# Norm weights per k tile on two engines, a running sum moved behind a K eviction, and V tiles drawn ahead of the memory attention, in the second layer of a two-layer trunk

## The chip, the cores and the metric

One core of a Trainium2 chip runs the whole program. The metric is the time of one execution on the device in microseconds (us), the median of three. Five instruction streams work side by side: TensorE (PE, with its weight loads as PEld), VectorE (DVE), ScalarE (ACT), GpSimd (POOL) and SyncE (SP), which issues the DMAs. Each takes its own instructions in order.

## The reference

Two layers over 1024 positions of width 1024. The change lies in layer B, whose front part computes this:

```python
h = rmsnorm(x, g_mix[l])
mem_k, mem_v = jnp.split(mem_n @ w_mem_kv[l], 2, axis=-1)
hk = rmsnorm(x, g_kv)
kvf = hk @ w_kvf                      # K (12 heads x 64), V (12 x 64), forget logits (12)
cum_logf = jnp.cumsum(jax.nn.log_sigmoid(f_logit), axis=1)
p = h @ w_in_b[l - N_A]               # FoX queries (12 heads) and memory queries (4 heads)
mix = forgetting_attention(q, k_sh, v_sh, cum_logf)
mem_o = memory_attention(q_mem, mem_k, mem_v)
x = x + jnp.concatenate([mix, mem_o], axis=-1) @ w_out[l]
x = x + conv_ffn(rmsnorm(x, g_ffn[l]), ...)
```

`rmsnorm(x, g)` scales by `g` along the width, which is the contracted dimension of each projection. So the norm weights can be multiplied into the weight matrix, and the row factor of the norm is applied to the result.

## The kernel before

Every operand of a float32 product is split into two parts, hi and lo, and a product is three matmuls: hi by hi, lo by hi, hi by lo (`mm3`, lines 108 to 110, and line 1111 for V). The width of 1024 is eight k tiles of 128 rows.

**Weights.** `load_w` (line 87) loads 128 x 1024 weights (for V 128 x 1040, half of a group of four heads) into one of two `raw` buffers. Where norm weights are given, one POOL multiply over the whole tile (line 99) applies them in place, ACT casts the product to hi (line 81) and DVE subtracts to get lo (line 82). Twenty loads in layer B do so: two memory-query tiles (`wqm`), six V halves (`wv`), six K tiles (`wk`), six Q tiles (`wq`).

**Order of the front part of layer B.** `normed` (line 178) splits x and, for each half of 512 positions, adds up squares, transposes the sum into columns by matmul (`st`, line 133), takes root and reciprocal (`sd` on ACT, `rs` on DVE, lines 140 and 142) and broadcasts the result back by matmul (`bc`, line 123), which ACT copies to `rb` (line 190). `st` and `bc` of both halves take the PSUM banks c2 and c3 in turn. `memattn(0)` projects the memory queries (`pq`, banks c0 and c1) and runs `mem_attention` (line 233): scale by `rb` (line 240), split (`bmq`, lines 246 and 247), scores (`ms`), softmax, transposes (`mt`) and values (`mo`).

**Fill.** Between those steps TensorE gets other work from a list: `mark` (line 290) pops steps from it at a given rate, `drain_fill(n)` pops n at once. During the memory attention the list holds 96 V steps (three groups of heads, eight token tiles each, four steps of six matmuls per tile, `vps`); each tile ends with an eviction by ACT and DVE (lines 1117 to 1120). Afterwards the list holds 192 K and Q steps (per pair of heads t: 8 K steps for the first half of the positions, 8 for the second, then 16 for Q), each of three matmuls; 32 of them are drained at once. For t = 0 the two halves use banks c0 and c1; from t = 1 on all use c0, so each half waits until the one before it is evicted by DVE (`bkc`, line 1170, and `bqc`, line 1172).

**Running sum.** The forget logits go through a chain of small DVE and ACT operations, are transposed (`lft`, line 1199), and summed along positions by one DVE scan (`bcum`, line 1204). ACT and DVE split the sum (`bch`, `bcl`, lines 1207 and 1208), four DMAs write it and its negative to memory, and `prep` loads them as extra rows of the score operands. After that, 20 more fill steps (`AHEAD`) are drained and the attention loop starts (`scores`, `values`: `fs`, `ft`, `fo`).

**Who sets the order.** The instructions are traced in the order of the program, and a scheduler that simulates the engines sorts each engine's stream; `issue_after(ins)` lets an instruction follow `ins` on its engine. So a change of the code also moves instructions that it doesn't name.

Of the kernel before, what the change touches and what calls it, by code (L numbers as in the profile page):

```python
# [8 lines left out]
F32 = mybir.dt.float32  # L9
# [3 lines left out]
ALU = mybir.AluOpType  # L13
AX = mybir.AxisListType

P = 128
# [14 lines left out]
VP = 260  # L31
# [20 lines left out]
class Trunk:  # L52
# [34 lines left out]
    def load_w(self, src, shape, gains=None, name="w", pools=None, lo_eng=None):  # L87

        nc = self.nc
        ph, pl = pools or ((self.main, "wh", None), (self.main, "wl", None))  # L90
        raw = self.main.tile([P] + shape, F32, tag="raw", name=f"{name}_raw", bufs=self.NRAW)
        nc.sync.dma_start(raw, src)
        hi = ph[0].tile([P] + shape, F32R, tag=ph[1], name=f"{name}_hi", bufs=ph[2])
        lo = pl[0].tile([P] + shape, F32R, tag=pl[1], name=f"{name}_lo", bufs=pl[2])
        if gains is None:
            self.split(hi, lo, raw, lo_eng=lo_eng)
        else:
            g = gains.rearrange("p (k o) -> p k o", o=1).to_broadcast([P] + shape)
            self.GENG(nc).tensor_tensor(raw, raw, g, op=ALU.mult)
            self.split(hi, lo, raw, lo_eng=self.LOENG(nc))  # L100
        return hi, lo

    def mm3(self, out, terms, start=True, stop=True):
# [930 lines left out]
    def layer_b(self):  # L1034
        nc, tc = self.nc, self.tc
# [3 lines left out]
        def pth(dt, nm):  # L1039
            return pc.tile([P, HS], dt, tag="pt", name=nm, bufs=6)  # L1040

        wqm = self.load_w(self.wib[CT], [KD, P], gains=self.vec("g_mix1", 0, KD), name="wqm0")
        xh, xl, rb, cols = self.normed("b", None, tmp1=lambda nm, w: pth(F32, nm))
# [4 lines left out]
        def unit(shape, dt, nm):  # L1048
            return self.main.tile(shape, dt, tag="x", name=f"b{nm}")

        def ptile(w=HS):
            return pc.tile([P, HS], F32, tag="ps", name="ps", bufs=4)[:, :w]

        def proj_half(w, u, hf, ks):
            wh, wl = w
            n = len(ks)
            self.mm3(u, [(wh[:, k], wl[:, k], xh[hf][k], xl[hf][k]) for k in ks],
                     start=ks[0] == 0, stop=ks[-1] == KD - 1)
# [7 lines left out]
        def memattn(ct):  # L1066
            w = wqm if ct == 0 else self.load_w(self.wib[CT + ct], [KD, P], gains=self.vec("g_mix1", 0, KD),
                                                name=f"wqm{ct}")
            hs = []
            for hf in range(2):  # L1070
                u = self.ps.tile([P, HS], F32, tag=f"c{hf}", name="pq")
                proj_half(w, u, hf, list(range(KD)))
                hs.append(u)
            o = [ptile(), ptile()]

            def put(e, hf, po):
                self.fold_rows(o[hf], po, e, self.nt("fr"))
                if e == 1:
                    nc.sync.dma_start(self.d_mix[CT + ct, :, hf * HS:(hf + 1) * HS], o[hf])

            self.mem_attention(hs, rb, ct, ks1, vs1, unit, pth, put, ("b2", "c2", "c3"), self.VMARKS)
# [8 lines left out]
        def load_v(pc_):  # L1090
            if pc_ < 3 and pc_ not in wv:
                wv[pc_] = [self.load_w(self.wv[pc_, u], [4, VP], gains=self.vec("g_kv", 4 * u, 4), name=f"wv{pc_}{u}",
                                       pools=((vp, "vh", 4), (vp, "vl", 4))) for u in range(2)]

        def v_steps(pc_):

            d = {}

            def step(i):
                t, kk = i // 4, i % 4  # L1100
                hf, ti = t // 4, t % 4
                if i == 0:
                    load_v(pc_ + 1)
                if kk == 0:
                    d["ps"] = self.ps.tile([P, VP], F32, tag=f"c{t % 2}", name="vps")
                ps = d["ps"]
                tsl = slice(ti * P, (ti + 1) * P)
                for k in (2 * kk, 2 * kk + 1):
                    wh, wl = wv[pc_][k // 4]
                    for j, (a, w) in enumerate(((xh, wh), (xl, wh), (xh, wl))):  # L1110
                        nc.tensor.matmul(ps, lhsT=a[hf][k][:, tsl], rhs=w[:, k % 4], start=k == 0 and j == 0,  # L1111
                                         stop=k == KD - 1 and j == 2)
                if kk == 3:
                    r = cols[hf][:, ti:ti + 1]
                    vo = vp.tile([P, 4, P], F32R, tag="vo", name="vo", bufs=3)
                    pv_ = ps[:, :MEM].rearrange("p (h d) -> p h d", h=4)
                    nc.scalar.activation(vo[:, :, :DH], pv_, AF.Copy, scale=r)
                    nc.vector.scalar_tensor_tensor(vo[:, :, DH:], pv_, r, vo[:, :, :DH].bitcast(F32),
                                                   op0=ALU.mult, op1=ALU.subtract)
                    nc.vector.scalar_tensor_tensor(fl[:, t, 4 * pc_:4 * pc_ + 4], ps[:, MEM:], r,  # L1120
                                                   self.bf[:, 4 * pc_:4 * pc_ + 4], op0=ALU.mult, op1=ALU.add)
                    nc.sync.dma_start(self.d_v[pc_, :, :, t], vo.bitcast(F32))
            return [lambda i=i: step(i) for i in range(32)]
# [12 lines left out]
        for e in range(2):  # L1136
            d = {n: pb.tile([P, S], F32R, tag=f"{n}{e}", name=f"{n}{e}") for n in ("q1", "q2", "k1", "k2")}
# [8 lines left out]
        def load(u):  # L1146
            t, n = u // 2, "kq"[u % 2]
            if t < CT and (t, n) not in ws:
                src, g = (self.wk, "g_kv") if n == "k" else (self.wib, "g_mix1")
                ws[t, n] = self.load_w(src[t], [KD, P], gains=self.vec(g, 0, KD), name=f"w{n}{t}")  # L1150
# [3 lines left out]
        def kq_steps(t):  # L1154

            d = kqv[t] = {}

            def step(i):
                n, hf, k = ("k", "q")[i // 16], i // 8 % 2, i % 8
                sl = slice(hf * HS, (hf + 1) * HS)  # L1160
                if i % 16 == 0:
                    load(2 * t + (n == "q") + 1)
                    d["w" + n] = ws.pop((t, n))
                    d[n] = unit([P, S], F32, n + "c")
                if k == 0:
                    d["u"] = self.ps.tile([P, HS], F32, tag="c1" if t == 0 and hf else "c0", name="pq")
                proj_half(d["w" + n], d["u"], hf, [k])
                if k == KD - 1:
                    if n == "k":
                        nc.vector.tensor_tensor(d[n][:, sl], d["u"], rb[:, sl], op=ALU.mult)  # L1170
                    else:
                        nc.vector.scalar_tensor_tensor(d[n][:, sl], d["u"], SCALE, rb[:, sl],
                                                       op0=ALU.mult, op1=ALU.mult)
            return [lambda i=i: step(i) for i in range(32)]
# [20 lines left out]
        lf = unit([NFOX, S], F32, "lf")  # L1195
# [5 lines left out]
        on = unit([NFOX, S], F32, "on")  # L1201
        nc.gpsimd.memset(on, 1.0)
        cum = unit([NFOX, S], F32, "cum")
        nc.vector.tensor_tensor_scan(cum, on, lf, 0.0, op0=ALU.mult, op1=ALU.add)
        ch = unit([NFOX, S], F32R, "ch")
        cl = unit([NFOX, S], F32R, "cl")
        nc.scalar.copy(ch, cum)
# [10 lines left out]
        def prep(t, e):  # L1218
            k, q = kqv[t]["k"], kqv[t]["q"]
            h = 2 * t + e  # L1220
            d = st[e]
            a, b = (slice(0, DH), slice(DH, P)) if e == 0 else (slice(DH, P), slice(0, DH))
            nc.vector.tensor_copy(d["q1"][a], q[a])
            nc.vector.tensor_copy(d["k1"][a], k[a])
            nc.gpsimd.tensor_tensor(d["q1"][b], q[a], d["q1"][a].bitcast(F32), op=ALU.subtract)
            self.dup2(d["k1"][b], d["k1"][a])
            nc.gpsimd.tensor_tensor(d["k2"][a], k[a], d["k1"][a].bitcast(F32), op=ALU.subtract)
            self.dup(d["q2"][a], d["q1"][a])
            e0 = DH if e == 0 else 0
            nc.sync.dma_start(d["q2"][e0:e0 + 2].bitcast(F32), self.d_c[h, 0:2])  # L1230
            nc.sync.dma_start(d["k2"][e0 + 2:e0 + 4].bitcast(F32), self.d_c[h, 2:4])
            vs = pb.tile([P, KD, P], F32R, tag="vsf", name="vsf", bufs=2)
            nc.sync.dma_start(vs.bitcast(F32), self.d_v[h // 4, :, h % 4])
            return vs
# [59 lines left out]
                    nc.tensor.matmul(po, lhsT=vs[:, j], rhs=pl[:, u], start=False, stop=j == 2 * I + 1)  # L1294
            self.fold_rows(o, po, e, self.nt("fr", 2 * P))

        self.drain_fill(self.AHEAD)
        vss = {(0, 0): prep(0, 0), (0, 1): prep(0, 1)}
        its = [(t, e, I) for t in range(CT) for e in range(2) for I in range(4)]
        pend = []  # L1300
# [125 lines left out]
    LAG = 2  # L1426
    VLAG = 3
    VRATE = 3.0
    GENG = staticmethod(lambda nc: nc.gpsimd)
    LOENG = staticmethod(lambda nc: nc.vector)  # L1430
    RATE = 0.8888888888888888
    LOOK = 1
    PREP = (5, 7)
# [135 lines left out]
```

## Time and profile before

| | us |
|---|---|
| median of three runs | 2347.88 |
| the runs | 2345.26, 2347.88, 2347.89 |
| the profiled execution | 2350.14 |
| its span, first to last instruction | 2348.3 |
| PE busy | 2261.3 (96%) |
| DVE, ACT, POOL busy | 1457.6, 1075.4, 1335.9 |
| mean granted TensorE clock | 0.987 of full |

The profiled execution took 1.84 us outside its span and lies 2.26 us above the median. All times in rows are us from the start of the span; durations in rows of single instructions are us, in rows of counts they are ns. A granted clock of 1.00 is 2.4 GHz, 0.50 is 1.2 GHz. A bracket at the end of a row is the time for which the engine sat idle before the instruction, and what it waited for.

### The profile page before, as it was taken

What the parts mean: (1) busy time and instruction counts of PE and PEld (TensorE: products, weight loads), DVE (VectorE), ACT (ScalarE), POOL (GpSimd) and SP (SyncE); (2) the same over time, 40 slices, a digit from 0 to 9 for tenths busy, and PEclk for the clock granted to TensorE, in tenths of its full rate; (3) what the DMA queues carried; (4) which work ended last, traced back from release to release, by engine and by line L of the source; (5) the groups of instructions that cost most, each with busy time, mean ns of one, the idle gap of its engine ahead of it and who ended that gap; (6) DMA issues with size and microseconds to landing.
All of it is one profiled execution on the core that took longest, in us unless ns stands there. A gap on an engine that the chain in (4) does not pass through costs nothing.

```text
span 2348.3 us, 29697 instructions
## 1 busy us (share of the span) xinstructions
PE 2261.3 (96%) x10970; PEld 1869.1 (80%) x10970; DVE 1457.6 (62%) x1995; ACT 1075.4 (46%) x1864; POOL 1335.9 (57%) x1003
## 2 busy tenths in 40 slices
PE   6999889999999999999998999999899999999998
PEld 6777668877878787888897888788788888778887
DVE  7479787766666653325645777866766666655225
ACT  6876746443434343223542666754443333343212
POOL 3676844566777776453423444614486767666533
PEclk9999989999999999999999999999999999999999
DMA  6100113222222235332432232433122222245322
GB/s 241 37 27 28 33 69 119 68 80 74 81 81 83 82 110 189 102 107 89 129 104 81 70 78 72 122 103 126 54 90 80 83 72 90 72 132 181 108 72 72
DMA packets 85281, 216.74 MB, mean 92 GB/s; under 512 B 9008, under 2 KB 29232, under 8 KB 85136
## 3 DMA queue, kind: packets, MB, share of 16 engines
q1 hardware_dynamic: 84992, 214.52, 28.7%
q8 instruction: 86, 1.41, 0.3%
q14 instruction: 59, 0.48, 0.1%
q10 hardware_dynamic: 144, 0.32, 0.0%
HBM read 156.94 MB, written 51.58 MB: 89 GB/s over the span
## 4 chain that ended last, share of the span: by engine, by line
PE 52%; DVE 4%; POOL 2%; issue 2%; DMA 2%; ACT 1%; DVEq 0%; ACTq 0%; POOLq 0%; SPq 0%
PE uY L345 7%; PE dn L109 7%; PE dn L108 6%; PE dn L110 6%; PE uX L345 5%; PE uV L345 5%; PE vps L1111 3%; PE pq L108 2%; PE pq L110 2%; PE pq L109 2%; DMA wd_raw<-in_wdn 1%; PE ft L1285 1%; PE fo L1294 1%; PE fo L1293 1%; PE fs L1249 1%
## 5 line engine op out<-in xcount | busy, mean ns | idle before, releaser
L345 PE MATMUL uY<-fT,fwh 128*128 128x512 f32 x1056 | 331.2, 394 | 5.9 <-DVE fuv L564 3.0
L109 PE MATMUL dn<-gl,wd_hi 128*128 128x512 f32 (+1 forms) x752 | 284.6, 379 | 0.5 <-POOL gl L82 0.5
L651 DVE TENSOR_TENSOR fx<-fx,dn 128x512 f32<-128x512 f32 (+1 forms) x176 | 111.2, 638 | 277.7 <-PE dn L110 276.3
L108 PE MATMUL dn<-gh,wd_hi 128*128 128x512 f32 (+1 forms) x752 | 280.7, 378 | 1.3 <-ACT fx L650 1.3
L110 PE MATMUL dn<-gh,wd_lo 128*128 128x512 f32 (+1 forms) x752 | 279.1, 375 | 0.0
L345 PEld LDWEIGHTS uY<-fT,fwh 128*128 128x128 f32 x1056 | 196.5, 188 | 55.8 <-DVE fuv L546 8.5
L345 PE MATMUL uX<-fB,fwh 128*128 128x512 f32 x704 | 223.0, 398 | 9.0 <-ACT fuv L521 9.0
L345 PE MATMUL uY<-fT,fwl 128*128 128x512 f32 x528 | 206.7, 391 | 0.0
L82 POOL TENSOR_TENSOR fwl<-wa,fwh 128x512 fp32r<-128x512 f32 x88 | 118.7, 1350 | 119.0 <-ACT fwh L81 119.0
L82 POOL TENSOR_TENSOR wd_lo<-wd_raw,wd_hi 128x1024 fp32r<-128x1024 f32 x44 | 108.0, 2461 | 127.5 <-ACT wd_hi L81 120.5
L345 PEld LDWEIGHTS uX<-fB,fwh 128*128 128x128 f32 x704 | 132.8, 190 | 42.0 <-ACT fuv L521 12.0
L108 PEld LDWEIGHTS dn<-gh,wd_hi 128*128 128x128 f32 x752 | 141.2, 188 | 30.0 <-ACT fx L650 1.7
L110 PEld LDWEIGHTS dn<-gh,wd_lo 128*128 128x128 f32 x752 | 141.0, 188 | 27.2
L109 PEld LDWEIGHTS dn<-gl,wd_hi 128*128 128x128 f32 x752 | 141.3, 188 | 25.8 <-POOL gl L82 0.9
L82 POOL TENSOR_TENSOR fwl<-wb,fwh 128x512 fp32r<-128x512 f32 x88 | 119.4, 1359 | 63.8 <-ACT fwh L81 63.0
L864 POOL TENSOR_TENSOR yp<-yp,ct 128x512 f32<-128x512 f32 x100 | 135.7, 1360 | 28.7 <-ACT ct L863 23.8
L82 POOL TENSOR_TENSOR gl<-g,gh 128x512 fp32r<-128x512 f32 x88 | 117.0, 1350 | 56.9 <-ACT gh L81 56.7
L82 POOL TENSOR_TENSOR fwl<-fs,fwh 128x512 fp32r<-128x512 f32 x88 | 118.3, 1346 | 52.9 <-ACT fwh L81 52.9
L345 PE MATMUL uX<-fB,fwl 128*128 128x512 f32 x352 | 138.5, 395 | 0.0
L345 PEld LDWEIGHTS uY<-fT,fwl 128*128 128x128 f32 x528 | 99.2, 188 | 22.4
L81 ACT CAST wd_hi<-wd_raw 128x1024 fp32r<-128x1024 f32 x44 | 45.6, 1050 | 152.4 <-issue 83.7
L345 PE MATMUL uV<-fB,fwh 128*128 128x512 f32 x352 | 111.5, 394 | 1.5 <-DVE fuv L529 1.5
(398 smaller groups left out, 6235.2 us busy)
## 6 DMA issues: line engine op xcount, KB each, us to landing
wb<-in_wup SPq DMA_DIRECT2D x44, 512.0 KB
wa<-in_wup SPq DMA_DIRECT2D x44, 512.0 KB
d_g<-fsg SPq DMA_DIRECT2D x44, 512.0 KB
wd_raw<-in_wdn SPq DMA_DIRECT2D x44, 512.0 KB
g<-d_g SPq DMA_DIRECT2D x44, 512.0 KB
d_x<-x SPq DMA_DIRECT2D x32, 256.0 KB
nxs<-d_x SPq DMA_DIRECT2D x32, 256.0 KB
wia_raw<-in_wia SPq DMA_DIRECT2D x14, 512.0 KB
```

Source lines behind the costliest of these rows:

```text
L81: nc.scalar.copy(hi, src)
L82: (lo_eng or nc.gpsimd).tensor_tensor(lo, src, hi.bitcast(F32), op=ALU.subtract)
L108: nc.tensor.matmul(out, lhsT=ah, rhs=bh, start=start and i == 0, stop=False)
L109: nc.tensor.matmul(out, lhsT=ah, rhs=bl, start=False, stop=False)
L110: nc.tensor.matmul(out, lhsT=al, rhs=bh, start=False, stop=stop and i == n - 1)
L345: mm = nc.tensor.matmul(out, lhsT=w[:, k], rhs=h[k], start=start and k == 0 and j == 0, stop=k == n - 1 and j == 2, skip_group_check=True)
L651: return nc.vector.tensor_tensor(self.x[m][:, sl], self.x[m][:, sl], ps, op=ALU.add)
L864: nc.gpsimd.tensor_tensor(y[:, hf], y[:, hf], c, op=ALU.add)
L1111: nc.tensor.matmul(ps, lhsT=a[hf][k][:, tsl], rhs=w[:, k % 4], start=k == 0 and j == 0, stop=k == KD - 1 and j == 2)
L1249: mm = nc.tensor.matmul(o, lhsT=d["q1"][:, qs], rhs=d["k1"][:, ksl], start=True, stop=False)
L1285: mm = nc.tensor.transpose(pt[:, u, P:], p1[:, j * P:(j + 1) * P], self.ident)
L1293: nc.tensor.matmul(po, lhsT=vs[:, j], rhs=ph[:, u], start=j == 0, stop=False)
```

## The change

`load_w` no longer multiplies the whole tile on POOL. For each k tile ACT computes hi with the norm weight as its scale (`split_gain`, line 168 before, 167 after) and DVE computes lo as x times weight minus hi (line 169 before, 168 after). Eight steps of the V fill, which are two tiles, are drained between the query projection and the memory attention, and the first two V tiles use banks c2 and c3. Eight K steps (the first half of t = 1) are drained before the running sum, and the scan is issued behind the eviction that ends them; 12 more steps follow the scan instead of 20.

```diff
         if gains is None:
             self.split(hi, lo, raw, lo_eng=lo_eng)
         else:
-            g = gains.rearrange("p (k o) -> p k o", o=1).to_broadcast([P] + shape)
-            self.GENG(nc).tensor_tensor(raw, raw, g, op=ALU.mult)
-            self.split(hi, lo, raw, lo_eng=self.LOENG(nc))
+            for k in range(shape[0]):
+                self.split_gain(hi[:, k], lo[:, k], raw[:, k], gains[:, k:k + 1])
         return hi, lo
...
                 hs.append(u)
+            if ct == 0:
+                self.drain_fill(8)
             o = [ptile(), ptile()]
...
                 if kk == 0:
-                    d["ps"] = self.ps.tile([P, VP], F32, tag=f"c{t % 2}", name="vps")
+                    d["ps"] = self.ps.tile([P, VP], F32, tag=f"c{t % 2 + 2 * (t < 2 and pc_ == 0)}", name="vps")
...
                     if n == "k":
-                        nc.vector.tensor_tensor(d[n][:, sl], d["u"], rb[:, sl], op=ALU.mult)
+                        self.last_k = nc.vector.tensor_tensor(d[n][:, sl], d["u"], rb[:, sl], op=ALU.mult)
...
         cum = unit([NFOX, S], F32, "cum")
-        nc.vector.tensor_tensor_scan(cum, on, lf, 0.0, op0=ALU.mult, op1=ALU.add)
+
+        self.drain_fill(8)
+        with self.issue_after(self.last_k.ins):
+            nc.vector.tensor_tensor_scan(cum, on, lf, 0.0, op0=ALU.mult, op1=ALU.add)
...
-        self.drain_fill(self.AHEAD)
+        self.drain_fill(self.AHEAD - 8)
...
-    GENG = staticmethod(lambda nc: nc.gpsimd)
-    LOENG = staticmethod(lambda nc: nc.vector)
```

What this does to the order of the engines is shown at three places. The first is PE at the end of the norm of layer B (`st` of the second half of the positions, its `bc`, the first scores `ms`). Before:

```order
L133 MATMUL st<-ones_69,sq 128x1 x4
L123 MATMUL bc<-ident,rs 128x128 x4
L259 MATMUL ms<-bks_8602,bmq 128x256
L260 MATMUL ms<-bks_8603,bmq 128x256
L259 MATMUL ms<-bks_8602,bmq 128x256
```

Now:

```order
L132 MATMUL st<-ones_69,sq 128x1 x4
L1112 MATMUL vps<-wv_hi,bh_8466 128x260
L1112 MATMUL vps<-wv_hi,bl_8482 128x260
L1112 MATMUL vps<-wv_lo,bh_8466 128x260
...
L1112 MATMUL vps<-wv_lo,bh_8473 128x260
L122 MATMUL bc<-ident,rs 128x128 x4
L258 MATMUL ms<-bks_8615,bmq 128x256
```

The 24 matmuls of the first V tile now stand between `st` and `bc`; eight `ms` follow `bc`, and then the second V tile. Before, the first V tile stood behind those eight `ms`.

The second place is ACT at the same time, where `sd` is the root that the second half's norm needs. Before:

```order
L152 ACTIVATE sq<-fx_6841 128x512
L81 CAST wv_hi<-wv_raw 128x1040
L190 COPY rb<-bc 128x512
L140 ACTIVATE sd<-st,eps_rms 128x4
L81 CAST wv_hi<-wv_raw 128x1040
```

Now:

```order
L151 ACTIVATE sq<-fx_6841 128x512
L167 ACTIVATE wv_hi<-wv_raw,vecs 128x260 x8
L189 COPY rb<-bc 128x512
L139 ACTIVATE sd<-st,eps_rms 128x4
L245 CAST bmq<-pq 64x512 x2
```

Both halves of the next V group (eight pieces) now stand ahead of `sd`; before it was one half.

The third place is DVE around the running sum. Before:

```order
L1223 CAST q_9931<-bqc 64x1024
L82 TENSOR_TENSOR wk_lo<-wk_raw,wk_hi 128x1024
L1200 COPY blf<-lft 12x512
L1204 SCALAR_TENSOR_TENSOR bcum<-bon,blf 12x1024
L1208 TENSOR_TENSOR bcl<-bcum,bch 12x1024
L1170 TENSOR_TENSOR bkc<-pq,rb 128x512 x2
```

Now:

```order
L1227 CAST q_9987<-bqc 64x1024
L168 SCALAR_TENSOR_TENSOR wk_lo<-wk_raw,vecs,wk_hi 128x128
L1201 COPY blf<-lft 12x512
L168 SCALAR_TENSOR_TENSOR wk_lo<-wk_raw,vecs,wk_hi 128x128 x4
L1171 TENSOR_TENSOR bkc<-pq,rb 128x512
L1208 SCALAR_TENSOR_TENSOR bcum<-bon,blf 12x1024
L1212 TENSOR_TENSOR bcl<-bcum,bch 12x1024
L1171 TENSOR_TENSOR bkc<-pq,rb 128x512
```

The first K eviction of t = 1 now stands ahead of the scan, the second behind `bcl`; the split of a later K tile is in pieces, the last four just ahead of the first eviction.

## Rows read from the trace of the kernel before

**Rows 1.** Stretches of 20 us: length, PE, PEld, DVE, ACT, POOL busy, granted clock, DMA.

```profile
1120.00:1140.00 20.00, 16.47 (x98) 15.42 (x97) 15.60 (x22) 11.08 (x25) 10.18 (x8) 0.83 0.32 103
1300.00:1320.00 20.00, 20.00 (x128) 17.14 (x127) 15.68 (x32) 11.72 (x27) 7.33 (x7) 1.00 0.31 77
```

**Rows 2.** PE in order of time, end of the norm: start, us, line, idle before.

```profile
1128.51 1.16 PE L123 MATMUL bc<-ident,rs 128*128 128x128 f32 x8 [2.45 <-DVE rs L142]
1130.35 0.58 PE L259 MATMUL ms<-bks,bmq 128*128 128x256 f32 x1 [0.69 <-DVE bmq L247]
1136.79 0.28 PE L1111 MATMUL vps<-wv_hi,bl 128*128 128x260 f32 x1
1136.91 0.28 PE L1111 MATMUL vps<-wv_lo,bh 128*128 128x260 f32 x1
```

**Rows 3.** The other engines in the same stretch, in order of time.

```profile
1122.19 4.48 POOL L99 TENSOR_TENSOR wv_raw<-wv_raw,vecs 128x1040 f32<-128x1040 f32 x2 [2.72 <-DMA wv_raw<-in_wv]
...
1125.34 0.58 ACT L190 COPY rb<-bc 128x512 f32<-128x512 f32 x1
1125.47 2.30 DVE L82 TENSOR_TENSOR wv_lo<-wv_raw,wv_hi 128x1040 fp32r<-128x1040 f32 x1 [0.58 <-ACT wv_hi L81]
1126.10 0.26 ACT L140 ACTIVATE sd<-st,eps_rms 128x4 f32<-128x4 f32 x1 [0.18 <-PE st L133]
```

**Rows 4.** PE in order of time around the running sum.

```profile
1271.52 0.79 PE L108 MATMUL pq<-bh,wk_hi 128*128 128x512 f32 x1 [6.44 <-DVE bkc L1170]
...
1279.40 0.28 PE L1250 MATMUL fs<-k,q 68*128 68x256 f32 x1
...
1280.44 0.47 PE L108 MATMUL pq<-bh,wq_hi 128*128 128x512 f32 x1 [0.44 <-DVE bkc L1170]
```

**Rows 5.** DVE, POOL and SP's queue around the running sum, in order of time.

```profile
1259.81 6.15 POOL L1225 TENSOR_TENSOR q<-bqc,q 64x1024 fp32r<-64x1024 f32 x2 [0.92 <-DVE q L1223]
1260.41 3.31 DVE L82 TENSOR_TENSOR wk_lo<-wk_raw,wk_hi 128x1024 fp32r<-128x1024 f32 x1
1264.42 3.67 DVE L1204 TENSOR_TENSOR_SCAN bcum<-bon,blf 12x1024 f32<-12x1024 f32 x1
1269.20 1.66 DVE L1208 TENSOR_TENSOR bcl<-bcum,bch 12x1024 fp32r<-12x1024 f32 x1 [1.11 <-ACT bch L1207]
1270.80 0.67 DVE L1170 TENSOR_TENSOR bkc<-pq,rb 128x512 f32<-128x512 f32 x1
...
1273.87 0.54 SPq L1231 DMA_DIRECT2D k<-d_c  x2
```

**Rows 6.** By tile: count, shortest, median, longest ns, first and last start.

```profile
L82 DVE TENSOR_TENSOR wk_lo<-wk_raw,wk_hi x6: 1205/1210/3307, 1176.0 to 1402.8; 128x1024 fp32r<-128x1024 f32 x6
L888 ACT ACTIVATE dg<-ident,wth x35: 388/396/407, 73.5 to 281.0; 128x128 fp32r<-128x128 f32 x35
L1225 POOL TENSOR_TENSOR q<-bqc,q x12: 2384/2695/3235, 1259.8 to 1515.9; 64x1024 fp32r<-64x1024 f32 x12
```

**Rows 7.** Groups by shape, first 20 us: count, busy us, mean ns, idle before.

```profile
L168 ACT ACTIVATE mh<-mem,vecs 128x256 fp32r<-128x256 f32 x8 | 3.4, 492 | 0.0
L169 DVE SCALAR_TENSOR_TENSOR ml<-mem,vecs,mh 128x256 fp32r<-128x256 f32 x8 | 3.3, 481 | 0.0
```

**Rows 8.** PE after two other waits, in order of time.

```profile
210.15 0.39 PE L259 MATMUL ms<-aks,amq 128*128 128x256 f32 x1 [2.62 <-ACT amp L265]
...
1666.37 0.71 PE L345 MATMUL uV<-fB,fwh 128*128 128x512 f32 x2 [1.46 <-DVE fuv L529]
```

**Rows 9.** Stretches behind waits (columns as in rows 1).

```profile
210.00:216.00 6.00, 5.85 (x21) 4.78 (x22) 5.83 (x7) 5.08 (x12) 5.84 (x8) 0.72 0.02 8
1130.00:1136.00 6.00, 5.65 (x26) 5.65 (x27) 3.56 (x6) 4.71 (x11) 3.72 (x2) 0.50 0.39 134
1668.00:1672.00 4.00, 3.93 (x18) 3.14 (x18) 1.70 (x2) 0.00 (x0) 4.00 (x4) 1.00 0.00 0
```

**Rows 10.** ACT in the attention loop: the cast of a Q tile.

```profile
1325.04 1.05 ACT L81 CAST wq_hi<-wq_raw 128x1024 fp32r<-128x1024 f32 x1
```

## The prediction

> **What bounds the kernel now.** I read the page first, for the busy share of each engine (TensorE, called PE, is the fullest), then stretches of 20 us to find where PE is not full, then each engine in order of time there. In the attention loop PE is busy for 20.00 of 20 us at a granted clock of 1.00, while ScalarE (ACT) has 11.72 and VectorE (DVE) 15.68 [rows 1]: what the change adds to ACT and DVE there is beside PE's work as long as nothing waits for it, and what it takes from GpSimd (POOL) there is worth nothing by itself. In the stretch at the end of the norm PE has 16.47 of 20 us and the clock 0.83 [rows 1]. So two holes in PE's stream are to be looked at.
>
> Hole A is the end of the norm [rows 2]: PE waits 2.45 us for `rs` and 0.69 for `bmq`. The other engines show why [rows 3]. POOL gets the first of the two weights halves at 1122.19 and multiplies them until 1126.7; ACT's `sd` starts at 1126.10, but DVE, which must then take the reciprocal `rs`, is in `wv_lo` from 1125.47 for 2.30 us. After the wait PE runs at a clock of 0.50 [rows 9]. Hole B is at the running sum: PE waits 6.44 us, from 1265.08 to 1271.52, and another 0.44 us before 1280.44, both for the K eviction `bkc` [rows 4]. On DVE, in order, stand `wk_lo` (3.31 us), the scan (3.67), a wait for `bch` (1.11), `bcl` (1.66), and only then `bkc` (0.67) [rows 5]. `wk_lo` takes 1.21 us elsewhere [rows 6]; here it runs beside POOL's two subtracts of 6.15 us [rows 5].
>
> **Prices.** On ACT a piece of 128x128 is nearest to `dg`, 0.39 us [rows 6]: eight are 3.1, against 1.05 for the one cast [rows 10]. A piece of 128x260 is nearest to `mh`, 3.4 busy us for eight, so 0.43 [rows 7]. On DVE `ml`, of the very form of the new pieces, gives 3.3/8 = 0.41 for 128x256 [rows 7]; a 128x128 piece lies between that and an eighth of `wk_lo`, 0.15 [rows 6], and I take the middle, 0.28 (eight are 2.2, against 1.21). One vps matmul of 260 columns follows the other by 0.12 us at full clock [rows 2], so 512 columns take 0.24.
>
> What a wait costs in clock is read from two others: after one of 2.62 us [rows 8] the clock was 0.72 for 6 us, a loss of 0.28 x 6 = 1.7; after one of 1.46 us [rows 8] it stayed at 1.00 [rows 9]. After hole A it was 0.50 for 6 us, a loss of 3.0 [rows 9]. I charge each new wait by the row that it is nearest to, with 0 and 3.0 as bounds.
>
> **Part A, V tiles ahead of the memory attention.** Before, from the start of `sd`, 1126.10, to the end of the first V tile, 1137.03 (0.12 behind the start of its last matmul), 10.9 us go by [rows 2, 3]. Now, for the same matmuls: x, then 24 V matmuls (24 x 0.12 = 2.9), `bc` (1.16 [rows 2]) and eight `ms` (8 x 0.12 = 1.0), so x + 5.0. x is PE's wait for bank c2, which is free when `sd` has read `st`. Ahead of `sd` on ACT now stand both V halves. POOL's second multiply followed the first without a gap (4.48 us for two), so the second half had landed by 1122.19 + 2.24 = 1124.4; four pieces (1.7), `rb` (0.58) and `sd` (0.26) [rows 3] make 1126.9, x = 0.8. That half, though, is loaded when DVE's pieces of the V half before it give back its buffer, eight of which take 8 x 0.41 = 3.3 instead of 2.4: x = 1.7, which I take. The lower bound is 0.7; the upper one adds what POOL made a `wv_lo` wait (2.30 against 1.21): 2.8. `rs`, `rb` and `bmq` then have the V matmuls to hide behind, 2.9 us. A wait of 1.7 is nearest to the row of 1.46, so no clock is charged. Gain: 10.9 - 5.0 - 1.7 = **4.2**.
>
> **Part B, the scan behind the eviction.** Before, from 1265.08 to 1280.44, 15.4 us. Now: y, the 24 matmuls of the second half (24 x 0.24 = 5.7), the wait for its eviction (0.7) and the 0.6 us of scores that stood from 1279.40 to 1280.00 [rows 4] and now come behind: y + 7.0. y is the wait for the first eviction. Four pieces of `wk_lo` stand ahead of it. If they wait out POOL's second subtract, that is over between 1265.2 (two of the median 2.695 [rows 6]) and 1265.96 [rows 5]; four pieces (1.1) and `bkc` (0.67) make 1267.0 to 1267.7, y = 1.9 to 2.7. I take 2.3; the bounds are 0.7 (the eviction alone) and 3.2 (pieces at 0.41). This is nearest to the 2.62 us wait: 1.7 of clock. Scan, `bch` and `bcl` (6.4 us as timed before) now lie beside the 5.7 us of matmuls, so up to 0.9 could show; the scan no longer meets a POOL subtract, so I take none. The chain goes on to the loads of the bias rows. From the start of the scan, 1264.42, to the end of their issue, 1274.41, it took 10.0 us [rows 5]; PE now comes to its first use 5.7 + 0.7 + 18 x 0.24 = 10.7 us behind `bkc`. That is hidden by little; nothing is charged. Gain: 15.4 - 7.0 - 2.3 - 1.7 = **4.4**.
>
> The trace alone doesn't say whether a DVE operation beside a POOL one waits or runs slowly. By the Trainium skill, SBUF — State Buffer, section "SBUF: two separate sides", the pair of ports is an exclusive lock, so a piece would wait for a whole subtract; were it shared, pieces spread over the subtract would be done before PE asks, y would be 0.7 and the gain 1.6 larger, before clock. The 3.31 us agree with either.
>
> **Part C, pieces everywhere.** POOL loses 20 multiplies of some 2 us each, which PE waits for in hole A alone. ACT gains 14 x (3.1 - 1.05) = 28.7 for K, Q and memory-query tiles and 6 x (4 x 0.43 - 1.05) = 4.0 for V halves, together 32.7 us; DVE some 1.0 us a tile. Five of these loads fall into the attention loop, where ACT has 8 us of 20 to spare [rows 1]. The cover is PE's queue of fill steps; if an exponential waits behind eight pieces, PE's transposes do next. Bounds: 0, and 5 x 2.05 = 10 if nothing hides. PE's 20.00 of 20 puts it near the first; I take a tenth, **-1.0**.
>
> A rule speaks against part C: by the Trainium skill, VectorE: DVE Perf Modes, section "The TRN2 errata", every operation that reads SBUF pays a fixed extra time, many small tiles pay it each, and tiles of at least 512 elements are advised. Its formula for ScalarE gives an estimate of 0.29 us for 128 elements, 2.35 for eight; `dg` [rows 6] is longer, and the row decides.
>
> **The sum.** 4.2 + 4.4 - 1.0 = 7.6. The profiled execution would go from 2350.14 to 2342.5. It lies 2.26 above the median; against the median of 2347.88 the forecast is **2340.3**. About 0.2%, 4.7 us, is what a measurement of this kernel can tell from no change: the bounds of faster and slower are 2343.2 and 2352.6.
>
> **Rivals.** *The clock holds and the waits are short*: x = 0.7, y = 0.7, no clock, C = 0. Then 10.9 - 5.0 - 0.7 = 5.2 and 15.4 - 7.0 - 0.7 = 7.7, 12.9 in all: 2335.0. For it: the clock's 1.00 after 1.46 us [rows 8, 9], and POOL, which loses work. Against: `sd` and `bkc` stand behind pieces.
>
> *The holes refill*: x = 2.8, y = 3.2, 3.0 of clock each. Then A gives 0.1, B 2.2, less 1.0: 1.3, so 2346.6. For it: what a DVE operation lost beside POOL, 2.1 us in `wk_lo` [rows 5, 6], and the 0.50 clock after hole A.
>
> *It does half of what it says*: eight drained steps are two V tiles, but only one stands before `bc`, the second behind `ms`. If `rs` is then as late as it was, A gives nothing: 4.4 - 1.0 = 3.4, 2344.5. Against: 2.9 us of matmuls more than before cover `rs`.
>
> *Slower, by ACT*: eight pieces are drawn ahead of an exponential or a V eviction in ACT's order, and PE waits for that. It decides from the point where PE sees 8.6 / 32.7 = 26% of the added ACT time; at 41% it is slower by over 0.2%. If half shows, 16.4 - 8.6 = +7.8: 2355.7. For it: ACT takes its instructions in order, and 1.05 us of a load become 3.1 in one block. Against: the spare time of ACT in the loop and PE's full stretches [rows 1].
>
> **How the numbers follow.** Forecast 0.48 (0.06 of it within 0.2%), clock holds 0.18, refilled 0.18, half 0.04, slower 0.12. Faster by over 0.2%: 0.42 + 0.18 = 0.60; within: 0.06 + 0.18 + 0.04 = 0.28; slower: 0.12. The range goes from the clock rival, 2335.0, to just above the refilled one, 2347.0; the slower case and the ends of the others, about 0.2, are left out.
>
> **What would show it.** Right: PE waits 1 to 2.5 us before the first `vps` behind `st`, put down to `sd`; none over 0.5 before `bc`; 1.5 to 3 us for the first `bkc` of t = 1, none near 6; `wq_lo` and `wk_lo` pieces of about 0.3 us; PE still 20.00 of 20 in the loop. Wrong: clocks of 0.5 behind both places (refilled), waits of PE for ACT's exponentials or V evictions (slower), a wait for the loads of the bias rows, or gaps in the loop that sum to more than a few us.

## The result and the profile after

The changed kernel takes 2351.97 us (median of 20 runs, 2347.12 to 2356.98) against 2347.82 us (20 runs, 2344.14 to 2351.35) on the same chip: a ratio of 1.0021, interval 1.0014 to 1.0027. It is slower by 0.2%, where 2340.3 and faster was forecast, and lies outside the range.

| | before | after |
|---|---|---|
| profiled execution, its span | 2350.14, 2348.3 | 2352.14, 2350.4 |
| PE busy | 2261.3 | 2259.6 |
| DVE, ACT, POOL busy | 1457.6, 1075.4, 1335.9 | 1476.9, 1097.7, 1290.7 |
| mean granted clock | 0.987 | 0.987 |

One execution scatters by some us: PE reaches the first memory-query matmul of layer B at 1111.76 us before and at 1107.88 after, though PE's order up to there is the same; most of it is a clock of 0.83 against 1.00 from 320 to 340 us, in layer A. So in the traces I compare the **front**: from the first memory-query matmul of layer B to the first of the output projection. It takes 404.4 us before (1111.76 to 1516.12) and 410.5 after (1107.88 to 1518.38), 6.1 more. In stretches of 50 us (columns as in [rows 1]), before:

```profile
1150.00:1200.00 50.00, 49.92 (x363) 46.97 (x362) 27.99 (x51) 24.09 (x55) 17.79 (x18) 1.00 0.44 129
1350.00:1400.00 50.00, 49.92 (x313) 42.76 (x312) 37.93 (x79) 30.32 (x66) 23.13 (x18) 1.00 0.30 75
```

After, the same stretches:

```profile
1150.00:1200.00 50.00, 46.10 (x320) 42.10 (x319) 31.63 (x81) 29.00 (x84) 5.11 (x11) 1.00 0.43 127
1350.00:1400.00 50.00, 48.14 (x288) 40.87 (x287) 37.83 (x83) 29.12 (x68) 19.61 (x16) 0.97 0.29 74
```

PE, full before in the memory attention (1150 to 1200) and in the loop, now stands for 3.9 and 1.9 us, and the clock has fallen in the loop.

**The holes shrank about as forecast.** PE in order of time after the change, as [rows 2, 4]:

```profile
1120.60 0.95 PE L132 MATMUL st<-ones,sq 128*128 128x1 f32 x8
1124.08 0.39 PE L1112 MATMUL vps<-wv_hi,bh 128*128 128x260 f32 x1 [2.53 <-ACT sd L139]
...
1128.78 0.28 PE L259 MATMUL ms<-bks,bmq 128*128 128x256 f32 x1
...
1264.39 0.50 PE L107 MATMUL pq<-bh,wk_hi 128*128 128x512 f32 x1 [2.13 <-DVE bkc L1171]
...
1272.63 0.47 PE L107 MATMUL pq<-bh,wq_hi 128*128 128x512 f32 x1 [0.88 <-ACT wq_hi L167]
```

Hole A: from the end of `st`, 1121.55, to the end of the same V tile, `bc` and scores, 1128.90, are 7.35 us, against 10.97 counted so before (1126.06 to 1137.03): 3.6 gained. Hole B: from 1262.26 (1264.39 - 2.13) to 1272.63, and 0.6 of scores that now come later, are 11.0 us against 15.4: 4.4 gained.

**New waits ate it.** Further waits of PE above 1 us that the kernel before has not, in order of time:

```profile
1168.80 0.50 PE L279 MATMUL mo<-mth,bvs 128*128 128x512 f32 x1 [1.08 <-ACT mth L277]
...
1185.96 0.47 PE L107 MATMUL pq<-bh,wqm_hi 128*128 128x512 f32 x1 [1.41 <-DVE fl L1121]
...
1196.55 0.35 PE L258 MATMUL ms<-bks,bmq 128*128 128x256 f32 x1 [1.04 <-ACT bmp L264]
...
1301.41 0.38 PE L1298 MATMUL fo<-pl,vsf 128*128 128x256 f32 x1 [1.72 <-DVE pl L1294]
...
1353.68 0.38 PE L1298 MATMUL fo<-pl,vsf 128*128 128x256 f32 x1 [1.81 <-DVE pl L1294]
...
1407.59 0.38 PE L1298 MATMUL fo<-pl,vsf 128*128 128x256 f32 x1 [1.81 <-DVE pl L1294]
```

What makes a wait for `pl` is in the other engines' order of time around the second one:

```profile
1348.60 0.60 DVE L168 SCALAR_TENSOR_TENSOR wk_lo<-wk_raw,vecs,wk_hi 128x128 fp32r<-128x128 f32 x2
1349.12 0.68 DVE L1227 CAST q<-bqc 64x1024 fp32r<-64x1024 f32 x1
1349.72 3.24 DVE L168 SCALAR_TENSOR_TENSOR wk_lo<-wk_raw,vecs,wk_hi 128x128 fp32r<-128x128 f32 x4
1352.89 0.15 DVE L1266 RECIPROCAL r<-sm 128x1 f32<-128x1 f32 x1
1352.97 0.66 DVE L1294 TENSOR_TENSOR pl<-ft,ph 128x512 fp32r<-128x512 f32 x1
...
1349.95 2.61 POOL L1229 TENSOR_TENSOR q<-bqc,q 64x1024 fp32r<-64x1024 f32 x1 [4.46 <-DVE q L1227]
```

The query cast (`q`) now stands between the pieces. It releases POOL's subtract at once, and the four pieces behind it take 3.24 us, as they end 0.4 us after POOL does (1349.95 + 2.61 = 1352.56); `pl` stands behind them. Before, the whole `wk_lo` of 1.21 us stood ahead of that cast:

```profile
1352.46 1.21 DVE L82 TENSOR_TENSOR wk_lo<-wk_raw,wk_hi 128x1024 fp32r<-128x1024 f32 x1
1353.59 0.68 DVE L1223 CAST q<-bqc 64x1024 fp32r<-64x1024 f32 x1
```

By tile, `wk_lo` shows how far a single piece can lie from the median (count, then shortest, median, longest ns):

```profile
L168 DVE SCALAR_TENSOR_TENSOR wk_lo<-wk_raw,vecs,wk_hi x48: 270/341/2452, 1163.3 to 1406.5; 128x128 fp32r<-128x128 f32 x48
```

A piece takes some 0.34 us and the next starts 0.26 behind it (two take 0.60 above). The longest, 2.45, and three steps of 0.26 are the 3.24 us: one piece of the four bears the whole wait, and the others are as short as elsewhere. This agrees with the Trainium skill, SBUF — State Buffer, section "SBUF: two separate sides", by which the pair of ports is an exclusive lock; at a shared rate every piece beside POOL would be longer.

### The profile page after: what moved, and what is told of

Read it like the earlier page. It is cut to its first block, busy times and chain, and to the rows that moved or that the text cites. A ratio compares the mean times of both kernels' runs of the same rounds, so it can differ in the third digit from the quotient of the medians.

```text
span 2350.4 us, 29930 instructions
## 1 busy us (share of the span) xinstructions
PE 2259.6 (96%) x10970; PEld 1866.6 (79%) x10970; DVE 1476.9 (63%) x2111; ACT 1097.7 (47%) x1980; POOL 1290.7 (55%) x983
## 3 DMA queue, kind: packets, MB, share of 16 engines
q8 instruction: 86, 1.41, 0.2%
## 4 chain that ended last, share of the span: by engine, by line
PE 53%; DVE 4%; ACT 2%; issue 2%; DMA 2%; POOL 1%; DVEq 0%; ACTq 0%; POOLq 0%; SPq 0%
PE uY L344 7%; PE dn L108 7%; PE dn L107 6%; PE dn L109 6%; PE uX L344 5%; PE uV L344 5%; PE vps L1112 2%; PE pq L107 2%; PE pq L109 2%; PE pq L108 2%; PE op L108 1%; PE op L107 1%; PE op L109 1%; DMA wd_raw<-in_wdn 1%; PE fo L1298 1%
## 5 line engine op out<-in xcount | busy, mean ns | idle before, releaser
L344 PE MATMUL uX<-fB,fwh 128*128 128x512 f32 x704 | 223.3, 398 | 9.0 <-ACT fuv L520 8.9
L344 PEld LDWEIGHTS uY<-fT,fwl 128*128 128x128 f32 x528 | 99.1, 188 | 22.3
L81 ACT CAST fwh<-wa 128x512 fp32r<-128x512 f32 x88 | 54.2, 618 | 126.6 <-PE uY L344 93.0
```

Source lines behind the costliest of these rows:

```text
L81: nc.scalar.copy(hi, src)
L344: mm = nc.tensor.matmul(out, lhsT=w[:, k], rhs=h[k], start=start and k == 0 and j == 0, stop=k == n - 1 and j == 2, skip_group_check=True)
```

## The experiments

Theory P: the pieces cost the time. Theory R: the early drains move waits to later stages. Each run is given with its front (404.4 before, 410.5 after) and its ratio to the kernel before. A front comes from one execution and scatters by some us, the ratio from all runs: where the two differ, the ratio says what a change is worth, and the trace only what waits for what.

**Each half of the change alone.** `e1_pieces`, on the kernel before:

```diff
-            self.GENG(nc).tensor_tensor(raw, raw, g, op=ALU.mult)
-            self.split(hi, lo, raw, lo_eng=self.LOENG(nc))
+            for k in range(shape[0]):
+                self.split_gain(hi[:, k], lo[:, k], raw[:, k], gains[:, k:k + 1])
```

> The kernel before with the pieces alone: norm weights per k tile on ScalarE and VectorE, no early V tiles, scan and drains as before. Theory P (the pieces cost the time: in the loop VectorE's pieces meet GpSimd's query subtract, in the memory attention ScalarE's pieces stand ahead of casts that TensorE waits for): the three waits of 1.8 us for pl in the loop are there, with a drop of the clock behind each, and the time is 2352 to 2360 us. Theory R (the early drains take fill from later stages and so move the waits there, the pieces are innocent): no such waits, 2344 to 2349 us.

Measured: 2357.16 us, ratio 1.0041 (1.0028 to 1.0053), front 414.4. The three waits for `pl` are there (1.74, 1.81, 1.81), holes A and B have 3.03 and 6.62 us. Taking POOL out of the norm did not shorten hole A by itself.

`e2_order`, on the changed kernel, is the reverse:

```diff
-            for k in range(shape[0]):
-                self.split_gain(hi[:, k], lo[:, k], raw[:, k], gains[:, k:k + 1])
+            g = gains.rearrange("p (k o) -> p k o", o=1).to_broadcast([P] + shape)
+            nc.gpsimd.tensor_tensor(raw, raw, g, op=ALU.mult)
+            self.split(hi, lo, raw, lo_eng=nc.vector)
```

> The changed kernel with the norm weights put back on GpSimd, whole tiles: the early V tiles and the moved scan alone. Theory P: no wait over 1 us in the loop or in the later memory attention, hole B as short as in the changed kernel or shorter (a gain of 4 to 6 us), hole A shorter than before by 3 to 5 us; 2338 to 2342 us. Theory R: the waits of the memory attention (1.1, 1.4, 1.0 us) and of the loop stay, 2350 to 2354 us.

Measured: 2336.88 us, ratio **0.9956** (0.9944 to 0.9969), front 393.6, the fastest of all and 1 us below the range of theory P. PE there, in order of time:

```profile
1124.77 0.39 PE L1113 MATMUL vps<-wv_hi,bh 128*128 128x260 f32 x1 [0.35 <-ACT sd L140]
...
1260.14 0.50 PE L108 MATMUL pq<-bh,wk_hi 128*128 128x512 f32 x1 [0.55 <-DVE bkc L1172]
...
1266.76 0.47 PE L108 MATMUL pq<-bh,wq_hi 128*128 128x512 f32 x1 [0.87 <-DVE bkc L1172]
```

Both holes are all but closed, and no wait for `pl` comes before 1490. Theory R falls. Added to this, the pieces cost 410.5 - 393.6 = 17 us of front, and by the ratios (1.0021 - 0.9956) 15 us; added to the kernel before they cost 10 by either.

**The two moves apart**, on the kernel before, with the weights on POOL. `e6_scan`:

```diff
-                        nc.vector.tensor_tensor(d[n][:, sl], d["u"], rb[:, sl], op=ALU.mult)
+                        self.last_k = nc.vector.tensor_tensor(d[n][:, sl], d["u"], rb[:, sl], op=ALU.mult)
...
+        self.drain_fill(8)
+        with self.issue_after(self.last_k.ins):
-        nc.vector.tensor_tensor_scan(cum, on, lf, 0.0, op0=ALU.mult, op1=ALU.add)
+            nc.vector.tensor_tensor_scan(cum, on, lf, 0.0, op0=ALU.mult, op1=ALU.add)
...
-        self.drain_fill(self.AHEAD)
+        self.drain_fill(self.AHEAD - 8)
```

> The kernel before with the moved scan and its drains alone (weights on GpSimd, no early V tiles). If the two moves do not depend on each other: the wait for the first eviction of t = 1 falls from 6.4 us to 0.6, its clock drop goes, the front of layer B is 6 to 7.5 us shorter than before, and the time is 2339 to 2342 us. If part of what the two moves gave together came from the V tiles' other timing: a gain of 2 to 5 us.

Measured: 2340.9 us, ratio 0.9971 (0.9959 to 0.9983), front 397.1: 7.2 less, hole B 0.55 us.

`e7_vahead`:

```diff
+            if ct == 0:
+                self.drain_fill(8)
...
-                    d["ps"] = self.ps.tile([P, VP], F32, tag=f"c{t % 2}", name="vps")
+                    d["ps"] = self.ps.tile([P, VP], F32, tag=f"c{t % 2 + 2 * (t < 2 and pc_ == 0)}", name="vps")
```

> The kernel before with the early V tiles alone (weights on GpSimd, scan as before). If the moves are independent: the wait for rs (2.45 us) becomes one of 0.4 us for sd, no clock drop at the end of the norm, up to the running sum 3 to 4.5 us less than before, hole B unchanged (6.4 us): 2343 to 2345 us.

Measured: 2343.57 us, ratio 0.9987 (0.9979 to 0.9996), front 399.5: 4.9 less, 3.8 of it up to the forget transposes; hole B 6.44. The moves add up to 12.1; together they gave 10.8. By the ratios they are 6.8 and 3.1 us, together 10.3.

**Pieces for V alone.**

```diff
-            for k in range(shape[0]):
-                self.split_gain(hi[:, k], lo[:, k], raw[:, k], gains[:, k:k + 1])
+            if name.startswith("wv"):
+                for k in range(shape[0]):
+                    self.split_gain(hi[:, k], lo[:, k], raw[:, k], gains[:, k:k + 1])
+            else:
+                g = gains.rearrange("p (k o) -> p k o", o=1).to_broadcast([P] + shape)
+                nc.gpsimd.tensor_tensor(raw, raw, g, op=ALU.mult)
+                self.split(hi, lo, raw, lo_eng=nc.vector)
```

> The changed kernel with pieces for the six V halves alone; K, Q and memory-query tiles are weighted on GpSimd as before. Theory P: as the kernel with the norm weights on GpSimd, 2337 to 2343 us; if GpSimd's multiply is what holds the start of the V tiles at the end of the norm, up to 2 us faster than that one, if ScalarE's V pieces ahead of sd hold it (2.5 us in the changed kernel), up to 2 us slower. Theory R: 2350 to 2354 us.

Measured: 2340.71 us, ratio 0.9969 (0.9956 to 0.9981), front 398.8, 5.2 more than `e2_order`. The wait for `sd` is 2.53 again, as in the changed kernel, but up to the forget transposes only 0.6 us more go by than in `e2_order` (142.6 against 142.0). The rest comes late in the loop, with a wait of 3.31 for `pl` at 1497.87. DVE and POOL ahead of it show why, each in order of time:

```profile
1492.36 4.33 DVE L1232 CAST q<-bqc 64x1024 fp32r<-64x1024 f32 x1
...
1492.20 1.27 POOL L82 TENSOR_TENSOR bmxl<-mr,bmxh 128x512 fp32r<-128x512 f32 x1
1493.45 0.37 POOL L234 TENSOR_SCALAR ps<-ps,r 128x128 f32<-128x128 f32 x1
1493.79 2.35 POOL L82 TENSOR_TENSOR wo_lo<-wo_raw,wo_hi 128x1024 fp32r<-128x1024 f32 x1
```

A query cast of 0.68 us elsewhere lasts here until POOL has done three operations without a gap; in `e2_order` the same cast took 1.75. No V piece stands there, so V's pieces don't hold this cast themselves; why POOL left no gap was not tried. POOL's multiply of V costs nothing once the tiles are ahead.

**The collision taken out of the loop.**

```diff
-            nc.gpsimd.tensor_tensor(d["q1"][b], q[a], d["q1"][a].bitcast(F32), op=ALU.subtract)
+            eng = nc.vector if e == 0 and t > 0 else nc.gpsimd
+            eng.tensor_tensor(d["q1"][b], q[a], d["q1"][a].bitcast(F32), op=ALU.subtract)
```

> The changed kernel, with GpSimd's query subtract of the first head of a pair moved to VectorE from the second pair on, so that no GpSimd operation meets the wk_lo pieces in the loop. If the two engines' collision makes the three waits of 1.8 us (each with some 1 us of clock), the four pieces take about 1.1 us instead of 3.2, the waits shrink to under 0.6 us and the time falls by 5 to 8 us, to 2344 to 2347. If ScalarE's longer block (2.45 us instead of 1.05) makes them, they stay, and the time is 2351 to 2354.

Measured: 2354.31 us, ratio 1.0028 (1.0017 to 1.0039), front 408.5: the sum is a miss. The waits for `pl` in the three pairs shrank to one of 1.03, but VectorE's own subtracts made new ones in the last pairs (2.21 and 1.99). The second lies behind the front, where from the first to the last matmul of the output projection 134.8 us go by, and 130.2 to 130.7 in every other run. So the next run left those out (`0 < t < 4`):

> As the run that moved the query subtract to VectorE, but for the second, third and fourth pair alone, where pieces and subtract meet; the last pairs keep GpSimd, as there VectorE's added work made waits of its own (2.2 and 2.0 us). If the collision makes the three waits, the front of layer B (from the memory-query projection to the first step of the output projection) gets 5 to 9 us shorter than in the changed kernel, and the time is 2343 to 2348 us. If the time that the first such run did not gain was due to something else in the loop, it stays at 2351 to 2355.

Measured: 2350.76 us, ratio 1.0013 (1.0005 to 1.0022), front 404.6, 5.9 less than the changed kernel. The time is above the range that was named: by the ratios 1.9 us are gained, and the two intervals overlap. VectorE there, in order of time:

```profile
1352.29 0.68 DVE L1227 CAST q<-bqc 64x1024 fp32r<-64x1024 f32 x1
1352.89 1.12 DVE L168 SCALAR_TENSOR_TENSOR wk_lo<-wk_raw,vecs,wk_hi 128x128 fp32r<-128x128 f32 x4
...
1354.02 0.66 DVE L1295 TENSOR_TENSOR pl<-ft,ph 128x512 fp32r<-128x512 f32 x1
```

The same four pieces behind the same cast take 1.12 us instead of 3.24, and `pl` follows 1.1 us behind the cast's end instead of 3.2. That the collision makes the waits is shown; what it is worth in time is not, from this run alone.

**The same in front of the running sum.** On top of that run:

```diff
+            with self.issue_after(self.last_k.ins if name == "wk2" else None):
                 for k in range(shape[0]):
                     self.split_gain(hi[:, k], lo[:, k], raw[:, k], gains[:, k:k + 1])
```

> As the run with the query subtract of three pairs on VectorE, and in addition the wk pieces that stood ahead of the first eviction of t = 1 are put behind the second. If the four pieces that GpSimd's subtract blocks make the wait before that eviction: it falls from 2.1 to 2.8 us to 0.6, the clock drop behind it goes, the stretch from the forget transposes to the first values shortens by 3 to 4.5 us against that run, to 2346 to 2348 us. If the eviction is late for another reason, it stays at 2349 to 2352.

Measured: 2345.59 us, ratio 0.9992 (0.9983 to 1.0001), front 401.9. The wait before the second half of K is 0.55 us, and from the forget transposes to the first values it is 28.1 us against 32.2: 4.1 less. The ratio fell by 0.0021 against `e8_qdve3`, 4.9 us, a little more than was expected. Both collisions taken out bring it from 1.0021 to 0.9992, 6.8 us, with intervals that don't meet. What blocked the first eviction in the changed kernel, and here, in order of time; first the changed kernel:

```profile
1261.06 2.67 DVE L168 SCALAR_TENSOR_TENSOR wk_lo<-wk_raw,vecs,wk_hi 128x128 fp32r<-128x128 f32 x4
1263.65 0.68 DVE L1171 TENSOR_TENSOR bkc<-pq,rb 128x512 f32<-128x512 f32 x1
1264.26 2.27 DVE L1208 TENSOR_TENSOR_SCAN bcum<-bon,blf 12x1024 f32<-12x1024 f32 x1
...
1260.24 2.56 POOL L1229 TENSOR_TENSOR q<-bqc,q 64x1024 fp32r<-64x1024 f32 x1 [0.63 <-DVE q L1227]
```

Then this run, where VectorE waits for the matmuls and not the other way round:

```profile
1262.79 0.69 DVE L1172 TENSOR_TENSOR bkc<-pq,rb 128x512 f32<-128x512 f32 x1 [3.80 <-PE pq L110]
1263.40 2.27 DVE L1209 TENSOR_TENSOR_SCAN bcum<-bon,blf 12x1024 f32<-12x1024 f32 x1
...
1269.92 2.18 DVE L169 SCALAR_TENSOR_TENSOR wk_lo<-wk_raw,vecs,wk_hi 128x128 fp32r<-128x128 f32 x8
```

**Which engine's pieces.** Three runs on the changed kernel: `e5a_plain` has a whole cast and a whole subtract and leaves the norm weights out, `e5b_actpieces` has pieces on ACT and a whole subtract (weights left out of lo), `e5c_dvepieces` a whole cast (weights left out of hi) and pieces on DVE.

```diff
-            for k in range(shape[0]):
-                self.split_gain(hi[:, k], lo[:, k], raw[:, k], gains[:, k:k + 1])
+            self.split(hi, lo, raw, lo_eng=nc.vector)
```

> The changed kernel with one cast and one subtract a tile and no norm weights at all (the multiplication is left out): neither GpSimd's multiply nor pieces. Theory P (the pieces' time on ScalarE and VectorE costs, GpSimd's multiply costs little): as the kernel with the weights on GpSimd or up to 2 us faster, 2334 to 2338 us. Rival Q (the early arrival of the weights, without GpSimd's multiply to spread them out, sets the waits): waits of 1 us stay in the memory attention, 2341 to 2348 us.

Measured: 2339.98 us, ratio 0.9973 (0.9964 to 0.9981), front 397.7. The time lies between the ranges of theory P and rival Q. The front is 4.1 longer than with POOL's multiply: waits of 0.88, 1.41 and 0.84 stand in the memory attention, so rival Q has a part.

```diff
             for k in range(shape[0]):
-                self.split_gain(hi[:, k], lo[:, k], raw[:, k], gains[:, k:k + 1])
+                nc.scalar.activation(hi[:, k], raw[:, k], AF.Copy, scale=gains[:, k:k + 1])
+            nc.vector.tensor_tensor(lo, raw, hi.bitcast(F32), op=ALU.subtract)
```

> The changed kernel with ScalarE's pieces, and one whole VectorE subtract a tile (of x and hi, so the norm weight is left out of lo). If ScalarE's pieces make the waits at the end of the norm (2.5 us for sd) and in the memory attention (1.1, 1.4, 1.0), these stay, the three of the loop go, and the time is 2341 to 2346 us. If VectorE's pieces make them all: 2335 to 2339.

Measured: 2339.47 us, ratio 0.9970 (0.9959 to 0.9980), front 397.3: as without pieces. `sd` makes PE wait 1.32; no other wait in the front is above 0.9.

```diff
+            nc.scalar.copy(hi, raw)
             for k in range(shape[0]):
-                self.split_gain(hi[:, k], lo[:, k], raw[:, k], gains[:, k:k + 1])
+                nc.vector.scalar_tensor_tensor(lo[:, k], raw[:, k], gains[:, k:k + 1], hi[:, k].bitcast(F32),
+                                               op0=ALU.mult, op1=ALU.subtract)
```

> The changed kernel with one whole ScalarE cast a tile (of x, so the norm weight is left out of hi), and VectorE's pieces. Six of the eight pieces stand ahead of the query's cast here, two behind: if the collision with GpSimd's subtract makes the loop's waits, they are there but shorter (1 to 1.8 us, the block lasts as long as the subtract), and the time is 2338 to 2345 us; the wait for sd is under 1 us. If ScalarE's pieces make all the waits: 2335 to 2339.

Measured: 2344.67 us, ratio 0.9994 (0.9985 to 1.0002), front 404.5: 6.8 more than without pieces. Two waits for `pl` of 1.80 and 1.83, 3.00 for the first `bkc`, and 2.18 for `sd`, though ACT's casts are whole: the wait for `sd` has to do with VectorE's pieces too. Against `e5a_plain`, ACT's pieces alone cost nothing, VectorE's 6.8, both 12.9; by the ratios nothing, 4.9 and 11.3. Both cost more than the two apart, and why was not tried.

**`sd` ahead of the V pieces.**

```diff
+            with self.issue_after(self.last_sd.ins if name.startswith("wv1") else None):
                 for k in range(shape[0]):
                     self.split_gain(hi[:, k], lo[:, k], raw[:, k], gains[:, k:k + 1])
...
-        nc.scalar.activation(sd[:, :nb], ps, AF.Sqrt, bias=eps, scale=1.0 / n)
+        self.last_sd = nc.scalar.activation(sd[:, :nb], ps, AF.Sqrt, bias=eps, scale=1.0 / n)
```

> The changed kernel, with the pieces of the second V group put behind sd on ScalarE. If the pieces, which wait for their loads, hold sd in front of the first V tile, that wait falls from 2.5 us to under 0.6 and the part up to the running sum gets some 2 us shorter (more where the clock dropped): 2346 to 2350 us in all. If the V tile waits for something else too (its own weights, the bank), the wait stays over 1.5 us, and 2350 to 2354.

Measured: 2352.3 us, ratio 1.0021 (1.0011 to 1.0030), front 404.9, and no gain in time; in the trace the wait is 0.35, and the part up to the forget transposes 3.1 us shorter than in the changed kernel. Over 11 runs from 2346 to 2357 us, these 3 us were not found again: the wait is explained, what it is worth is not.

## Why the prediction was wrong

**Hole A** (4.2): the mechanism held. x was 2.53 instead of 1.7, inside its bounds, and no clock was lost in the profiled execution: 3.6. ACT shows why x is as it is, in order of time:

```profile
1121.68 1.72 ACT L167 ACTIVATE wv_hi<-wv_raw,vecs 128x260 fp32r<-128x260 f32 x4 [0.78 <-DMA wv_raw<-in_wv]
1123.30 0.56 ACT L189 COPY rb<-bc 128x512 f32<-128x512 f32 x1
1123.77 0.26 ACT L139 ACTIVATE sd<-st,eps_rms 128x4 f32<-128x4 f32 x1
```

The last four pieces wait for their load, and `sd` stands behind them; the prediction read that from the order. `e9_sdfirst` confirms it.

**Hole B** (4.4): 4.4 measured, y 2.13 against 2.3, and the clock fell behind it to 0.62 from 1266 to 1270, a loss of 1.5 (1.7 taken). Four pieces waiting out POOL's subtract was right. But y was taken as a price of the scan's move, though the pieces made it: without them (`e6_scan`) it is 0.55 and the move gives 7.2, of which 5.2 by the first values.

**Part C** (-1.0) failed, in the step "PE's 20.00 of 20 puts it near the first; I take a tenth". From the trace of the changed kernel: up to the forget transposes the front is 0.8 us longer though hole A gave 3.6 and the norm 0.6, so the memory attention lost 5.0; from the first values to the output projection it lost 7.3. Some 12 us, beyond the upper bound of 10. That bound only counted ACT's time in the loop, for five loads where the trace of before has six (the last `wq` at 1425.7), and nothing for the memory attention.

The front by stage, in us, shows what was lost where. The four runs below it have nearly the same matmuls in each stage; in the kernel before eight more, about 1 us of work, lie behind the first values, so the loop lost nearer 8:

| | to the forget transposes | to the first values | to the output projection |
|---|---|---|---|
| before | 145.8 | 33.5 | 225.1 |
| `e2_order`: POOL multiplies | 142.0 | 28.3 | 223.3 |
| `e5a_plain`: no weights | 146.5 | 28.0 | 223.1 |
| changed kernel: pieces | 146.6 | 31.5 | 232.4 |
| `e10_wk2late`: both collisions out | 148.3 | 28.1 | 225.5 |

What the pieces add in the running sum (3.2) and in the loop (9.1) goes, but for 2.2, when the two collisions are taken out. What is lost in the memory attention stays, and it is there without any piece: PE's waits between the first V tile and the forget transposes add up to 3.7 us in `e5a_plain`, 3.8 in the changed kernel and 1.2 in `e2_order`.

Two things were missed. First, the lock was applied to the place where it was seen in the trace of before and not to the loop, where the changed order put a cast, and so POOL's subtract, among the pieces. The rows had the prices: 3.31 against 1.21 [rows 5, 6], and a median of 2.7 us for POOL's subtract [rows 6]; but the prediction asks for the new order at the running sum alone, not in the loop. Second, the idle share of ACT was taken as cover; the wait came on DVE, with 2 us of block just ahead of `pl`.

The prices of the pieces alone were not at fault: eight on ACT take 2.45 us (3.1 taken), eight on DVE 2.17 to 2.19 without a collision (2.2 taken), and ACT's busy time grew by 22.3 us, not by 32.7. For ACT the estimate from the Trainium skill, VectorE: DVE Perf Modes, section "The TRN2 errata", 2.35, was nearer than my row.

**The rivals.** "Slower, by ACT" had the sign and the place, TensorE waiting in the loop, at a share of 12/32.7 = 37% of the ACT time that it added up, but not the engine: ACT's pieces alone cost nothing in `e5b_actpieces`. "POOL loses multiplies that PE waits for in hole A alone" fell with `e1_pieces` and `e2_order`: with POOL's multiply back, hole A is shorter (0.35). The other rivals are about the two holes alone, which gave 3.6 and 4.4 where 4.2 and 4.4 were forecast, so none of them explains the result.

**What stays open.** The waits of 1.41 and about 1 us in the memory attention come without POOL's multiply even where nothing is in pieces (`e5a_plain`), but not where only one engine has pieces (`e5b_actpieces`, `e5c_dvepieces`). So neither the missing multiply nor pieces as such make them by themselves: the weights are ready at other times, and the engines' order is another. Which of the two makes them was not tried, and with it the cause of the 5.0 us there stays open.

## What to carry to other kernels

A long operation cut into pieces lets others in between: look in the new order for what now stands among the pieces, and whom it releases. Where two engines block each other for a whole instruction, ask of every moved or split operation what runs on the other engine at that moment; a fully busy bottleneck engine and idle time elsewhere say nothing about it. And run the parts of a change apart: here two of three were worth 10 us, and the third cost more than that once they were in.

## What was not expected of the hardware

The clock behind equal waits differs from execution to execution. PE waits 2.53 us for `sd` in the changed kernel and 2.52 in `e4_qdve`, then runs the same matmuls. Of the two stretches from the wait on, first the changed kernel:

```profile
1120.00:1126.00 6.00, 3.47 (x31) 3.38 (x31) 4.66 (x11) 3.87 (x11) 0.00 (x0) 1.00 0.64 189
1126.00:1132.00 6.00, 6.00 (x53) 6.00 (x52) 3.19 (x6) 4.21 (x9) 0.00 (x0) 1.00 0.27 95
```

Then `e4_qdve`:

```profile
1120.00:1126.00 6.00, 3.48 (x24) 3.39 (x24) 4.68 (x11) 3.92 (x11) 0.00 (x0) 0.77 0.59 185
1126.00:1132.00 6.00, 6.00 (x37) 6.00 (x37) 1.99 (x5) 1.60 (x3) 0.00 (x0) 0.66 0.13 52
```

In the changed kernel a wait of 1.81 us was followed by a clock of 0.57 (1354 to 1358), one of 1.72 by 1.00 (1301 to 1307). So what a wait costs in clock can't be read from one row by its length, as the prediction did. It may also widen the scatter of the runs, which nothing here tests.
